# A decoder step on one core: a shared operand slot, two feed-forward tiles kept on chip, one pair of fetches issued later

## The chip, the cores and the metric

The kernel is one program on 1 core of a Trainium2 chip. The metric is the device time of a run in microseconds (us). Its engines are PE (matmuls), ACT and DVE (element-wise work), POOL (some element-wise work, and the DMA queue for transfers that accumulate) and SP (the DMA queue for loads). Every engine carries out its own instructions in order, and waits on semaphores for the others.

## The reference

One layer of a decoder over 512 prompt tokens and 64 sample tokens, `D_MODEL` 1024, everything in float32. The first half (projection, short convolution, windowed attention, mixing) is not touched. The second half, the feed-forward part with `D_FF` 2816, is:

```python
h2 = _rmsnorm(x, norm2_g) * (1.0 + sc2) + sh2
a, val = jnp.split(h2 @ w_up, 2, axis=-1)
ac, new_ffn = _causal_conv(a, ffn_buf, ffn_conv_w)
x = x + g2 * ((jax.nn.gelu(ac, approximate=False) * val) @ w_down)
```

## The kernel before, in words

Channels lie on the 128 partitions and the 576 tokens (`NT`) along the free axis. The 2816 feed-forward channels are 22 tiles of 128. For each tile m the "up" job makes the gate and the value, and their product t, a 128x576 tile of float32 (288 KB). The "down" jobs multiply those tiles by `w_down` and add to the residual.

A float32 product is done in three passes with numbers split into a high and a low part: high x high, high x low, low x high. The high part is an ACT copy into a rounded type, the low part the difference. Up jobs 4 to 21 and most down jobs are "pairs" (`pair_product`): two outputs, two halves of the tokens (a: columns 0 to 287, b: 288 to 575) and two halves of the contraction are done in seven products in place of eight. For this the operands are summed and subtracted first. In PE's queue the seven run one after the other as X, Z, Y, X, Y, Z, Y, after the three PSUM banks that they fill. An up pair has 84 matmuls of 288 columns, a down pair 63.

What stands beside the products is written out by hand: `steps[n]` is a list of small functions that are called after product n - 1 (`steps[0]` before the first), and PE, ACT, DVE and POOL keep this program order. The order of SP's queue, and the placing of tiles in buffers, are found at build time from a simulated timeline. The weights of the next pair are prepared in these steps. Of its four operand parts A, B, C and D, the low half of B and D is made by a POOL DMA that adds the raw weights to the negated high part (in rows: `wlo<-raw` for B and `wl<-s` for D); all else is done by ACT and DVE. In a down pair (k0, 0), the weight work is `sums1` (DVE: `s<-raw,raw`, then `raw<-raw`), `bh` (ACT: `whi<-raw`), `al` (DVE), `bl` and so on.

The order of the jobs: up 4 to 10; the four down pairs (0, 0), (0, 2), (0, 4), (0, 6), which use tiles 0 to 5; up 11 to 16; the down pairs (6, 0) to (6, 6), which use tiles 6 to 11; up 17 to 21; then the rest of down. The operands of a group of down pairs are made in the up jobs before it, two tiles (one k pair) at a time, by `RawOperands`: `sums` (DVE, three operations on the tiles), `first`, `second`, `third` (ACT, high parts) and `first_low` and so on (DVE). `third` of the third k pair runs at the start of (k0, 0). The seventh product's operand, `n4`, is only 288 columns wide. So `third` takes two slots for it, one for high and one for low, and two k pairs share them; the third k pair is alone in a second pair of slots and fills half of each.

"Slots" are one pool of 58 buffers of 128x576 float32 (`A_BUFS`). A tile gets a buffer that another tile had, and its first writer then waits for the last user of that one. The tiles in `KEPT` stay in their slots until a down job uses them. The others are written to DRAM (`away`) by a POOL DMA in the step `high`, and fetched again by an SP DMA (`fetch`): 10 tiles go away and 10 come back. For the last up job before a group of down pairs (`up_last`, tiles 10 and 16) the convolution, GELU and product run in down pairs (k0, 2) and (k0, 4).

The functions that the change touches:

Of the kernel before, what the change touches and what calls it, by code (L numbers as in the profile page):

```python
# [11 lines left out]
F32R = mybir.dt.float32r  # L12
# [15 lines left out]
PAIRED = 6  # L28
PLAIN_AT, LAST_AT = 12, 16
CHUNKS = {0: 10, 6: 16}  # L30
KEPT = (0, 1, 2, 3, 4, 5, 11, 17, 18, 19, 20, 21)
LATE = 2
ROWS_AHEAD = 5
PLAIN = (0, 1, 2, 4, 5, 6)
# [42 lines left out]
def step_kernel(ctx: ExitStack, tc: tile.TileContext, ins: dict, outs: list):  # L77
# [15 lines left out]
    def nm(s):  # L93
        cnt[0] += 1
        return f"{s}{cnt[0]}"

    def slot(s, dt=F32, shape=None):
        return ap_.tile(shape or [P, NT], dt, tag="a", name=nm(s))
# [4 lines left out]
    def aux():  # L103
        return pa.tile([P, 512], F32, tag="aux", name=nm("aux"))
# [3 lines left out]
    class InOrder:  # L108


        def __init__(self, engine):
            self.engine = engine
# [134 lines left out]
    class PairOperands:  # L247
# [21 lines left out]
        def high(self):  # L269
            made, (h0, l0), (h1, l1) = self.made, *self.x  # L270
            self.th, self.tl = slot("th", F32R), slot("tl", F32R)
            act.activation(self.th, self.t, AF.Copy)
            if self.kp % 2 == 0:
                made["n4"] = slot("nh", F32R), slot("nl", F32R)
            a, b = slice(0, HT), slice(HT, NT)
            at = (a, b)[self.kp % 2]
            nh, nl = made["n4"]
            self.nh, self.nl = nh[:, at], nl[:, at]
            act.activation(self.nh, self.r[0][:, a], AF.Copy)
            for name, hi, lo, c in (  # L280
                ("x00", h0, l0, a), ("n3", h0, l0, b), ("x10", h1, l1, a), ("x11", h1, l1, b),
                ("n1", self.th, self.tl, a), ("t2", self.th, self.tl, b), ("n4", nh, nl, at),
            ):
                made.setdefault("op", {}).setdefault(name, []).append((hi[:, c], lo[:, c]))
# [89 lines left out]
    class RawOperands:  # L374

        def __init__(self, r0, r1, made):
            self.r0, self.r1, self.made = r0, r1, made
            made.setdefault("op", {})  # L380

        def put(self, name, hl, c):
# [34 lines left out]
        def third(self):  # L417
            a, b, made = slice(0, HT), slice(HT, NT), self.made
            self.x1 = slot("xh", F32R), slot("xl", F32R)
            act.activation(self.x1[0], self.r1, AF.Copy)  # L420
            self.put("x10", self.x1, a)
            self.put("x11", self.x1, b)
            n = len(made["op"].get("n4", []))
            if n % 2 == 0:
                made["n4"] = slot("nh", F32R), slot("nl", F32R)
            at = (a, b)[n % 2]
            self.n4 = tuple(x[:, at] for x in made["n4"])
            act.activation(self.n4[0], self.r0[:, a], AF.Copy)
            self.put("n4", made["n4"], at)

        def third_low(self):
            self.low(self.x1, self.r1)
# [463 lines left out]
    made = {}  # L896
# [15 lines left out]
    for i in (3, 4):  # L912
        a = aux()
# [24 lines left out]
    def queries(t, ps=None, scale=HD**-0.5):  # L938
# [53 lines left out]
        op=ALU.mult,  # L992
# [488 lines left out]
    for at, m in enumerate(PLAIN):  # L1481
# [25 lines left out]
        if at == 1:  # L1507
            a = aux()
# [329 lines left out]
    class FfnTile:  # L1838
# [43 lines left out]
        def high(self):  # L1882
            if self.m in KEPT:
                kept[self.m] = self.t
# [128 lines left out]
    made2, made_d, kept = {}, {k0: {} for k0 in (*CHUNKS, LAST_AT)}, {}  # L2013
# [75 lines left out]
    ops_d, fs, ops, up_last = {}, {}, {}, {}  # L2089

    def raw_op(k0, kp, *names):
        def f():
            at = k0 + 2 * kp
            if at not in ops_d:
                ops_d[at] = RawOperands(kept.pop(at), kept.pop(at + 1), made_d[k0])
            for name in names:
                getattr(ops_d[at], name)()
        return f

    def fetch(*ms):  # L2100
        def f():
            for m in ms:
                kept[m] = slot("cy")
                nc.sync.dma_start(kept[m], away[m])
        return f
# [36 lines left out]
    order, first_ops = [], {}  # L2142
# [18 lines left out]
                                7: [lambda k0=k0: up_last[k0].high()]},  # L2161
        })
    calls = lambda f, *xs: [lambda x=x: f(x) for x in xs]
    first_ops["down", (0, 6)] = {4: [fetch(6, 7)]}
    first_ops["up", 12][3] = [fetch(8, 9)]
    first_ops["up", 14][3] = [fetch(10)]
    first_ops["up", 17] = {2: [fetch(12, 13)]}
    for at, m in ((18, 12), (19, 14), (20, 16)):
        first_ops["up", at] = {
            2: [fetch(*((14, 15), (16,), ())[at - 18])], 4: calls(down_high, m), 5: calls(down_low, m),  # L2170
            6: calls(down_high, m + 1), 7: calls(down_low, m + 1),
        }
    first_ops["up", 21] = {
# [5 lines left out]
    for n, at in enumerate(order):  # L2179
# [7 lines left out]
        if n + 2 < len(order):  # L2187
            kind, m = order[n + 2]
# [176 lines left out]
```

## Time and profile before

| what | value |
|---|---|
| median of 3 runs | 954.85 us (953.62 to 957.12) |
| the profiled execution, its own time | 955.27 us |
| its span, first to last instruction | 953.5 us |
| mean granted clock of PE | 0.996 |
| PE busy | 936.5 us, 98% of the span |
| DVE, ACT, POOL busy | 739.7, 600.5, 199.8 us |
| DMA | 166.74 MB, of it 50.58 MB on POOL's queue (q0) and 114.41 MB on SP's (q1) |

Times in rows are in us from the first instruction. A row of the timeline gives the start, the duration, engine and line, operation, `out<-in` by the names of the tiles and, in brackets, how long the engine had been idle before it and what ended that. Most operations carry line 116, since one helper records them; so they are told apart by their tiles. In the timeline the up jobs 4 to 10 end at 687.3, the first four down pairs run to 722.9, up 11 to 16 from there to some 790, and the second four down pairs to some 824.

### The profile page before, as it was taken

What the parts mean: (1) busy time and instruction counts of PE and PEld (TensorE: products, weight loads), DVE (VectorE), ACT (ScalarE), POOL (GpSimd) and SP (SyncE); (2) the same over time, 40 slices, a digit from 0 to 9 for tenths busy, and PEclk for the clock granted to TensorE, in tenths of its full rate; (3) what the DMA queues carried; (4) which work ended last, traced back from release to release, by engine and by line L of the source; (5) the groups of instructions that cost most, each with busy time, mean ns of one, the idle gap of its engine ahead of it and who ended that gap; (6) DMA issues with size and microseconds to landing.
All of it is one profiled execution on the core that took longest, in us unless ns stands there. A gap on an engine that the chain in (4) does not pass through costs nothing. (4 is left out here: it accounts for less than half of the span.)

```text
span 953.5 us, 19148 instructions
## 1 busy us (share of the span) xinstructions
PE 936.5 (98%) x7227; PEld 901.4 (95%) x7227; DVE 739.7 (78%) x1395; ACT 600.5 (63%) x1158; POOL 199.8 (21%) x426
## 2 busy tenths in 40 slices
PE   7999999999999999999999999999999999999996
PEld 5799999898999989999889999999999999999996
DVE  4788988875866767876677688888888889877965
ACT  5474768656665446875335567577766776677574
POOL 2222120101111011210001231122243233421131
PEclk9999999999999999999999999999999999999998
DMA  9984233516545768899884832368679877986643
GB/s 281 329 252 109 70 101 98 157 70 151 141 130 171 248 217 214 213 248 291 278 289 122 184 102 67 96 137 198 164 153 233 207 169 167 228 211 151 143 97 105
DMA packets 190032, 166.74 MB, mean 175 GB/s; under 512 B 9177, under 2 KB 162973, under 8 KB 189651
## 3 DMA queue, kind: packets, MB, share of 16 engines
q1 hardware_dynamic: 172210, 114.41, 40.3%
q0 software_dynamic: 17440, 50.58, 24.8%
q8 instruction: 57, 0.93, 0.4%
q10 hardware_dynamic: 288, 0.52, 0.1%
q14 instruction: 37, 0.30, 0.1%
HBM read 116.84 MB, written 15.02 MB: 138 GB/s over the span
## 5 line engine op out<-in xcount | busy, mean ns | idle before, releaser
L116 ACT ACTIVATE whi<-raw 128x1024 fp32r<-128x1024 f32 (+3 forms) x198 | 195.4, 996 | 35.7 <-DVE raw L116 18.0
L116 DVE TENSOR_TENSOR wlo<-raw,whi 128x1024 fp32r<-128x1024 f32 (+3 forms) x153 | 176.1, 1156 | 33.9 <-ACT whi L116 33.4
L116 POOL DMA_DIRECT2D wlo<-raw x45 | 39.0, 866 | 207.2 <-PE mm L116 96.2
L116 DVE TENSOR_TENSOR raw<-raw 128x512 f32<-128x512 f32 (+1 forms) x104 | 69.2, 665 | 3.4
L116 PE MATMUL aux<-2h,whi 128*128 128x288 f32 (+2 forms) x232 | 63.5, 294 | 0.0
L116 PE MATMUL aux<-2l,whi 128*128 128x288 f32 (+2 forms) x232 | 63.5, 295 | 0.0
L116 PE MATMUL mm<-hh,whi 128*128 128x256 f32 (+2 forms) x264 | 60.4, 304 | 0.5 <-ACT hh L116 0.5
L116 PE MATMUL mm<-hl,whi 128*128 128x256 f32 (+2 forms) x264 | 57.3, 297 | 0.0
L116 PE MATMUL mm<-hh,wlo 128*128 128x256 f32 (+2 forms) x264 | 55.4, 295 | 0.0
L116 PE MATMUL aux<-hl,whi 128*128 128x288 f32 (+1 forms) x196 | 53.3, 298 | 0.0
L116 PE MATMUL aux<-hh,whi 128*128 128x288 f32 (+1 forms) x196 | 53.2, 297 | 0.0
L116 POOL DMA_DIRECT2D wl<-s x41 | 35.6, 867 | 71.4 <-ACT wl L116 53.6
L116 ACT ACTIVATE mm<-aux 128x288 f32<-128x288 f32 x49 | 19.5, 397 | 46.7 <-PE aux L116 46.6
L116 ACT ACTIVATE wlo<-whi 128x1024 fp32r<-128x1024 f32 (+1 forms) x45 | 45.4, 1009 | 0.4
L116 PEld LDWEIGHTS mm<-hh,whi 128*128 128x128 f32 x264 | 43.8, 189 | 1.5 <-ACT hh L116 1.0
L116 PEld LDWEIGHTS mm<-hl,whi 128*128 128x128 f32 x264 | 44.1, 188 | 0.9 <-DVE hl L116 0.9
L116 PEld LDWEIGHTS aux<-2l,whi 128*128 128x128 f32 x232 | 43.6, 188 | 0.0
L116 PEld LDWEIGHTS mm<-hh,wlo 128*128 128x128 f32 x264 | 43.6, 188 | 0.0
L116 PEld LDWEIGHTS aux<-2h,whi 128*128 128x128 f32 x232 | 43.5, 188 | 0.0
L116 PE MATMUL aux<-2h,wlo 128*128 128x288 f32 (+2 forms) x232 | 42.1, 295 | 0.0
L1034 ACT ACTIVATE s<-s,nmx 128x256 f32<-128x256 f32 (+1 forms) x72 | 34.0, 477 | 9.6 <-DVE nmx L1028 8.9
L116 ACT ACTIVATE aux<-mm 128x288 f32<-128x288 f32 x52 | 20.6, 396 | 30.6 <-PE mm L116 29.5
(420 smaller groups left out, 3119.2 us busy)
## 6 DMA issues: line engine op xcount, KB each, us to landing
raw<-in_w_in SPq DMA_DIRECT2D x52, 512.0 KB, 4.8
raw<-in_w_up SPq DMA_DIRECT2D x44, 512.0 KB, 4.1
wlo<-raw POOLq DMA_DIRECT2D x34, 512.0 KB, 4.8
ada<-in_w_ada SPq DMA_DIRECT2D x64, 256.0 KB, 5.4
raw<-in_w_down SPq DMA_DIRECT2D x44, 192.0 KB, 3.4
ad<-in_w_ada SPq DMA_DIRECT2D x32, 256.0 KB, 6.2
wl<-s POOLq DMA_DIRECT2D x30, 256.0 KB, 4.3
sg_dram<-sg POOLq DMA_DIRECT2D x16, 288.0 KB, 4.3
```

Of the source, the lines that this page charges most:

```text
L116: done = getattr(self.engine, name)(*args, **kwargs)
L1034: nc.scalar.activation(s[x // 2][:, x % 2, :w], s[x // 2][:, x % 2, :w], AF.Exp, bias=nmx[:, x : x + 1], accum_out=den[:, x : x + 1],)
```

## The change

Three edits. `third` gives the operand `n4` of the third k pair one slot of its own, high part in columns 0 to 287 and low part in 288 to 575 of it, in place of two half-used slots. Tiles 10 and 16 join `KEPT`: their writes to DRAM and their fetches (in up 14 and in up 19) go. The fetch of tiles 6 and 7 moves from step 4 to step 6 of down pair (0, 6), and the `sums` that use them move from step 2 to step 4 of up 11.

```diff
-KEPT = (0, 1, 2, 3, 4, 5, 11, 17, 18, 19, 20, 21)
+KEPT = (0, 1, 2, 3, 4, 5, 10, 11, 16, 17, 18, 19, 20, 21)
...
             n = len(made["op"].get("n4", []))
-            if n % 2 == 0:
-                made["n4"] = slot("nh", F32R), slot("nl", F32R)
-            at = (a, b)[n % 2]
-            self.n4 = tuple(x[:, at] for x in made["n4"])
+            if self.alone:
+                x = slot("nh", F32R)
+                self.n4 = x[:, a], x[:, b]
+            else:
+                if n % 2 == 0:
+                    made["n4"] = slot("nh", F32R), slot("nl", F32R)
+                self.n4 = tuple(x[:, (a, b)[n % 2]] for x in made["n4"])
             act.activation(self.n4[0], self.r0[:, a], AF.Copy)
-            self.put("n4", made["n4"], at)
+            made["op"].setdefault("n4", []).append(self.n4)
...
-                ops_d[at] = RawOperands(kept.pop(at), kept.pop(at + 1), made_d[k0])
+                ops_d[at] = RawOperands(kept.pop(at), kept.pop(at + 1), made_d[k0], kp == PAIRED // 2 - 1)
...
-    first_ops["down", (0, 6)] = {4: [fetch(6, 7)]}
+    first_ops["down", (0, 6)] = {6: [fetch(6, 7)]}
+    first_ops["up", 11][4] = first_ops["up", 11].pop(2)
     first_ops["up", 12][3] = [fetch(8, 9)]
-    first_ops["up", 14][3] = [fetch(10)]
...
-            2: [fetch(*((14, 15), (16,), ())[at - 18])], 4: calls(down_high, m), 5: calls(down_low, m),
+            2: [fetch(*((14, 15), (), ())[at - 18])], 4: calls(down_high, m), 5: calls(down_low, m),
```

How it moves instructions and their waits. In the rows below a name ends in the number of its tile, and brackets hold the semaphores that an instruction waits on: an engine's name, DMASW0 to 7 for POOL's transfers, DMAHW0 to 7 for SP's.

First DVE and ACT at the start of down pair (0, 0). Here `cy1376` is tile 9, whose write to DRAM signals on DMASW1; `nl1388` is the low part of the third k pair's `n4`, `s` and `raw` are the sums of the next pair's weights, and `p5` is the scratch into which ACT copies the second product of (0, 0). DVE before, and DVE after:

```order
L116 TENSOR_TENSOR nl1388_8807<-cy1268_8025,nh1387_8806 128x288 [waits DVE_49,Activation_49]
L116 TENSOR_TENSOR s31391_8824<-raw1357_8642,raw1358_8645 128x384 [waits DMAHW2_49,DMAHW0_49,DMASW1_49]
L116 TENSOR_TENSOR raw1358_8645<-raw1358_8645 128x384 [waits DMAHW3_49,DVE_49]
L116 TENSOR_TENSOR wlo1390_8822<-raw1357_8642,whi1389_8821 128x768 [waits DMAHW1_49,Activation_49]
L116 TENSOR_TENSOR raw1357_8642<-raw1357_8642,raw1358_8645 128x384 [waits DMASW4_49,DVE_49]
```

```order
L116 TENSOR_TENSOR nh1387_8806<-cy1268_8025,nh1387_8806 128x288 [waits DMASW0_49,Activation_49]
L116 TENSOR_TENSOR s31390_8823<-raw1357_8642,raw1358_8645 128x384 [waits DMAHW2_49,DMAHW0_49,DVE_49]
L116 TENSOR_TENSOR raw1358_8645<-raw1358_8645 128x384 [waits DMAHW3_49,DVE_49]
L116 TENSOR_TENSOR wlo1389_8821<-raw1357_8642,whi1388_8820 128x768 [waits DMAHW1_49,Activation_49]
L116 TENSOR_TENSOR raw1357_8642<-raw1357_8642,raw1358_8645 128x384 [waits DMASW4_49,DVE_49]
```

The order is the same; the low part now lies in the slot of the high part, and `s` no longer waits on DMASW1 but only on an earlier DVE instruction. ACT at the same place, before and after:

```order
L116 ACTIVATE mm1382_8800<-aux1381_8799 128x288 [waits PE_49]
L116 ACTIVATE whi1389_8821<-raw1357_8642 128x768 [waits DMAHW1_49,DMAHW0_49]
L116 COPY p51384_8802<-aux1383_8801 128x288 [waits DVE_49,PE_49]
L116 ACTIVATE whi1392_8838<-raw1358_8645 128x768 [waits DMAHW3_49,DVE_49]
L116 ACTIVATE aux1383_8801<-mm1382_8800 128x288 [waits PE_49,Activation_49]
```

```order
L116 ACTIVATE mm1382_8800<-aux1381_8799 128x288 [waits PE_49]
L116 ACTIVATE whi1388_8820<-raw1357_8642 128x768 [waits DMAHW1_49,DMAHW0_49]
L116 COPY p51384_8802<-aux1383_8801 128x288 [waits DMASW1_49,PE_49]
L116 ACTIVATE whi1391_8837<-raw1358_8645 128x768 [waits DMAHW3_49,DVE_49]
L116 ACTIVATE aux1383_8801<-mm1382_8800 128x288 [waits PE_49,Activation_49]
```

The wait on DMASW1 now stands at ACT's copy of the second product, in the buffer that tile 9 had.

Then SP around the fetch of tiles 6 and 7 (`cy<-away`), between the raw weights of up 12 and up 13, before and after:

```order
L155 DMA raw1437_9145<-in_w_up 128x8x128 [waits DMAHW3_49,DMASW6_49,DMAHW6_49,DVE_49,Activation_49]
L155 DMA raw1438_9147<-in_w_up 128x8x128 [waits DVE_49]
L2104 DMA cy1447_9204<-away_7376 128x576 [waits DMASW0_49,DVE_49,DMAHW0_49,PE_49,Pool_49]
L2104 DMA cy1448_9206<-away_7376 128x576 [waits DMAHW1_49,DMASW3_49,PE_49]
L155 DMA raw1455_9255<-in_w_up 128x8x128 [waits DMAHW2_49,DMASW1_49,DMAHW5_49,DVE_49,Activation_49]
```

```order
L155 DMA raw1436_9143<-in_w_up 128x8x128 [waits DMAHW3_49,DMASW6_49,DMAHW6_49,DVE_49,Activation_49]
L155 DMA raw1437_9145<-in_w_up 128x8x128 [waits DVE_49]
L2107 DMA cy1452_9239<-away_7376 128x576 [waits DMAHW0_49,DMASW0_49,PE_49]
L2107 DMA cy1453_9241<-away_7376 128x576 [waits DMASW5_49,DMASW3_49,DMAHW1_49,DVE_49,Pool_49]
L155 DMA raw1454_9253<-in_w_up 128x8x128 [waits DMAHW2_49,DMASW0_49,DMAHW5_49,DVE_49,Activation_49]
```

In SP's own queue the fetches stand where they stood. Their buffers are others, and so their waits: tile 6 waits for a matmul, tile 7 for DVE and POOL operations that read the buffer's former tile. In the built program the PE wait of tile 6 is for the second matmul of the third product of (0, 6), the DVE wait of tile 7 for the second multiply of tile 10 (`cy<-p,y`), and the DMASW waits of both for older transfers.

Last POOL at the same place, before and after; `away<-cy1436` is the write of tile 10, `wlo` the transfer of B for the weights of up 11:

```order
L116 TENSOR_TENSOR rt1435_9127<-p51424_9037,modT_186 128x64 [waits DVE_49]
L116 TENSOR_TENSOR x11070_6533<-x11070_6533,rt1435_9127 128x64 [waits Pool_49]
L116 DMA away_7376<-cy1436_9130 128x576 [waits DMASW0_49,DVE_49]
L116 DMA wlo1446_9168<-raw1420_9032 128x1024 [waits DMASW4_49,DMASW1_49,DMAHW5_49,PE_49,Activation_49]
L1235 MEMSET pad1457_9259 128x2 [waits PE_49]
```

```order
L116 TENSOR_TENSOR rt1434_9126<-p51423_9036,modT_186 128x64 [waits DVE_49]
L116 TENSOR_TENSOR x11070_6533<-x11070_6533,rt1434_9126 128x64 [waits Pool_49]
L116 DMA wlo1445_9166<-raw1419_9031 128x1024 [waits DMASW4_49,DMASW0_49,DMAHW5_49,PE_49,Activation_49]
L1238 MEMSET pad1456_9257 128x2 [waits DVE_49]
L1860 COPY pad1456_9257<-stF_6334 128x8x2
```

The write of tile 10 is gone from in front of B's transfer.

More of the change, by code (lines that the diff above doesn't have):

```diff
@@ L374, in step_kernel, with __init__ @@
     class RawOperands:
-        def __init__(self, r0, r1, made):
-            self.r0, self.r1, self.made = r0, r1, made
+        def __init__(self, r0, r1, made, alone=False):
+            self.r0, self.r1, self.made, self.alone = r0, r1, made, alone
             made.setdefault("op", {})
```

## The prediction

> **What bounds the kernel now.** I read the page first, then what PE waited for, then the stages, then the timeline around each wait.
>
> ```profile
> PE 936.5 (98%) x7227; PEld 901.4 (95%) x7227; DVE 739.7 (78%) x1395; ACT 600.5 (63%) x1158; POOL 199.8 (21%) x426
> ```
>
> PE is busy for 936.5 of 953.5 us, and the change leaves its matmuls as they are. So it can gain only idle time of PE, and only in the feed-forward part. What PE waited for between 545 and 930 us:
>
> ```profile
> PE mm L116 <- ACT aux L116: 1.8, 1, 1.8
> PE aux L116 <- DMA wlo<-raw: 0.6, 1, 0.6
> ```
>
> Two waits, once each, are all. The busy time by stage says where (columns: PE, PEld, DVE, ACT, POOL busy, clock, DMA share, GB/s): the first four down pairs, up 11 to 16, and the second four down pairs.
>
> ```profile
> 687.30:722.90 35.60, 33.76 (x255) 33.52 (x254) 31.41 (x54) 24.98 (x42) 14.11 (x26) 1.00 0.74 183
> 722.90:790.00 67.10, 66.54 (x503) 66.31 (x502) 56.12 (x98) 47.99 (x78) 20.26 (x45) 1.00 0.82 194
> 790.00:826.00 36.00, 36.00 (x273) 36.00 (x272) 33.89 (x58) 25.41 (x43) 14.89 (x28) 1.00 0.79 186
> ```
>
> The first stage lacks 1.84 us, the second 0.56, the third, which does the same work on other tiles, nothing. The clock is full in all three. The most that the change can give is therefore 1.84 + 0.56 = 2.40 us, a quarter of a per cent. I call 0.5% (4.8 us) the least that a measurement of this kernel tells from no change.
>
> **The first wait: one slot fewer in (0, 0).** The chain of waits, then DVE and ACT at this place:
>
> ```profile
> 686.14 5.52 DMA away<-cy
> ...
> 689.19 0.45 DVE L116 TENSOR_TENSOR nl<-cy,nh 128x288 fp32r<-128x288 f32 x1
> 691.68 0.56 DVE L116 TENSOR_TENSOR s<-raw,raw 128x384 f32<-128x384 f32 x1 [2.04 <-DMA away<-cy]
> 692.27 0.56 DVE L116 TENSOR_TENSOR raw<-raw 128x384 f32<-128x384 f32 x1
> ...
> 689.87 0.40 ACT L116 COPY p<-aux 128x288 f32<-128x288 f32 x1
> 692.86 0.84 ACT L116 ACTIVATE whi<-raw 128x768 fp32r<-128x768 f32 x1 [2.60 <-DVE raw L116]
> 693.61 0.39 ACT L116 ACTIVATE aux<-mm 128x288 f32<-128x288 f32 x1
> ...
> 694.06 0.40 PE L116 MATMUL mm<-xh,wh 128*128 128x288 f32 x1 [1.84 <-ACT aux L116]
> ```
>
> Tile 9 is written to DRAM from 686.14 to 691.66. DVE's sum `s` gets its buffer and waits 2.04 us for it; `raw` comes after `s`, ACT's `whi` after `raw`, ACT's `aux` after `whi`, and PE needs `aux`. With the shared slot the order rows show `s` free of that transfer: the buffer that the low half of `n4` had taken goes to `s`. But the wait for tile 9 isn't gone. The next tile that asks for a buffer, `p5`, gets tile 9's, and ACT's copy `p<-aux`, which started at 689.87, now waits for the same landing. Behind it in ACT's queue stand `whi` and `aux`, so PE still waits for them, by a shorter way. Step by step on the old times: `s` follows `nl` at 689.66 and `raw` ends near 690.8, long enough ahead. The copy starts at 691.68, the instant at which DVE got the buffer. What follows such a copy on ACT is read at another place, where nothing is waited for:
>
> ```profile
> 717.08 0.39 ACT L116 COPY p<-aux 128x288 f32<-128x288 f32 x1
> 717.35 1.07 ACT L116 ACTIVATE wlo<-whi 128x1024 fp32r<-128x1024 f32 x1
> ```
>
> Start to start that is 0.27; I take 0.3. So `whi` starts at 691.98 in place of 692.86, `aux` 0.75 later as before (692.86 to 693.61), and PE 0.45 after that (693.61 to 694.06), at 693.18. The gain is 694.06 - 693.18 = 0.88, less an estimated 0.02 for one wait more in ACT's queue: 0.86. Of the 1.84 some 0.98 stays, now under ACT's copy. Nothing ahead of this place changes, so the landing should stand where it stood. Bounds: 0, if ACT resumes much later than DVE did, and 1.84, if tile 9 lands 1.8 us sooner. I take the value between, as the rows of this very place give it.
>
> **The second wait: B of up 11.** PE stops after 8 of the 12 matmuls of the second product, since the low part of B hasn't landed:
>
> ```profile
> 725.32 0.29 PE L116 MATMUL aux<-tl,whi 128*128 128x288 f32 x1
> 726.17 0.53 PE L116 MATMUL aux<-th,wlo 128*128 128x288 f32 x2 [0.56 <-DMA wlo<-raw]
> ...
> 718.73 7.40 DMA wlo<-raw
> ...
> 716.96 0.81 SPq L2104 DMA_DIRECT2D cy<-away  x2
> 717.12 0.38 DVE L116 TENSOR_TENSOR cy<-p,y 128x224 f32<-128x224 f32 x1
> 717.80 0.60 POOL L116 DMA_DIRECT2D away<-cy  x1 [0.79 <-DVE cy L116]
> ```
>
> PE would have gone on at 725.6; B, issued at 718.73, lands at 726.12. Ahead of it stand the two fetches (SP, 716.96) and the write of tile 10 (POOL, 717.80). What the two queues moved from 717.8 to 721.0, then from 721.0 to 726.2 (packets, MB, share of the engines):
>
> ```profile
> q1 hardware_dynamic: 1101, 0.77, 89.1%
> ...
> q0 software_dynamic: 343, 1.05, 88.7%
> q1 hardware_dynamic: 163, 0.31, 15.4%
> ```
>
> Until 721.0 no packet of POOL's queue moves at all; then it moves 1.05 MB in 5.2 us, 0.2 MB a us, first tile 10, then B. Two edits act on this. The write of tile 10 (128x576 float32, 0.295 MB) goes: 0.295 / 0.2 = 1.5 us off B's landing. The fetches are to come behind B, and there the order rows say otherwise. Nothing on SP waits for B: tile 6 now needs a matmul of about 717.1, tile 7 the multiply that ends at 717.50. They issue at some 717.2 and 717.6 in place of 716.96 and 717.4, and still ahead of B. So I give that edit nothing. B then lands at 726.12 - 1.5 = 724.6, a us before PE needs it, and the 0.56 us go. The twin of this place in the second group has the write (tile 16) and no fetch:
>
> ```profile
> 819.14 0.61 POOL L116 DMA_DIRECT2D away<-cy  x1 [1.09 <-DVE x L116]
> 819.75 0.89 POOL L116 DMA_DIRECT2D wlo<-raw  x1
> ...
> wlo<-raw POOLq DMA_DIRECT2D x1, 512.0 KB, 5.3
> ```
>
> B takes 5.3 us there, so without fetches ahead it would be even safer. Bounds: 0 to 0.56; a landing 0.56 us sooner is enough, so I take 0.56.
>
> A rule speaks against this term. The Trainium skill ("SBUF — State Buffer", section "SBUF: two separate sides", its warning on DVE) says that GpSimd can't write the descriptors of its own transfers while DVE runs an operation that takes the port they share, so that such a transfer looks slow without any traffic in its way. By that rule B's 7.4 us would be DVE's doing, tile 10's write would not matter, and the sum below would be 0.86 in place of 1.42. The twin, with the same DVE work beside it and no fetches, took 5.3, which the rule doesn't explain; I keep the traffic.
>
> **What costs nothing.** Two writes and two fetches fewer, 1.2 of 166.74 MB, none of which PE waited for but tile 10's. The `sums` in up 11 change places with DVE's two `raw` sums:
>
> ```profile
> 726.99 0.45 DVE L116 TENSOR_TENSOR tw<-cy 128x288 f32<-128x288 f32 x1
> ...
> 727.90 0.46 DVE L116 TENSOR_TENSOR tw<-cy,tw 128x288 f32<-128x288 f32 x1
> ...
> 728.99 0.69 DVE L116 TENSOR_TENSOR raw<-raw 128x512 f32<-128x512 f32 x1
> 731.86 0.52 DVE L116 TENSOR_TENSOR pad<-mm,p 128x224 f32<-128x224 f32 x2 [2.17 <-ACT xh L116]
> ...
> 733.17 0.29 PE L116 MATMUL mm<-nh,whi 128*128 128x288 f32 x1
> ```
>
> The five operations end at 729.7 either way, and DVE idles 2.17 us behind them. Tiles 10 and 16 hold a slot longer. The place where that is nearest to costing is (6, 0): ACT's copy `p<-aux` there waits, after the change, for tile 15's write, as its twin waits for tile 9's.
>
> ```profile
> 792.93 0.40 ACT L116 COPY p<-aux 128x288 f32<-128x288 f32 x1
> ...
> 789.18 0.58 POOL L116 DMA_DIRECT2D away<-cy  x1 [0.96 <-DVE cy L116]
> ...
> away<-cy POOLq DMA_DIRECT2D x1, 288.0 KB, 3.1
> ```
>
> It lands at 792.3, 0.6 us before the copy. That cover is thin: a write that takes 5.5 us, as tile 9's did, would land at 794.7, and the copy be 1.8 us late, with up to that at PE.
>
> **Sum.** 955.27 - 0.86 - 0.56 = 953.85 us for the profiled execution. That one lies 0.42 above the median of 954.85, so against the median: 953.4 us.
>
> **Rivals.** (1) Both waits go, 2.40 us: 952.4 us. For it: the same kind of write took 3.1 us at 789.18, and tile 9 has to land within 3.7 us of its issue. Against: nothing ahead of it changes. (2) Only the first gain: B is slow for a cause on POOL's or DVE's side, or the fetches alone make it late. Then 0.86, 954.0 us. Against: POOL's queue demonstrably moves tile 10 first. (3) Slower: SP holds the fetches behind B on the chip, as the change's words have it. Then they are issued near 726.1, and a transfer between the slots and `away` lasts up to 7.5 us:
>
> ```profile
> DMA to landing us min/median/max: 3.1/5.2/7.5
> ```
>
> They land at 733.6; the `sums` (1.37 us) and `pad` (0.52) follow, to 735.5, and PE, which starts the next product at 733.17, is 2.4 us late. Net 1.0 us slower: 955.8 us. It decides for slower once tile 7 lands after some 732.6 (731.2, from where PE waits at all, and 1.4 that the rest gains). Against: SP's rows have no wait on B. (4) Only the slot does nothing: ACT resumes as late as DVE did and only B's wait goes, 0.56: 954.3 us. For it: `p5` takes the wait over; against: the copy stands later in the chain than `s`, with two DVE sums cut out.
>
> **How the numbers follow.** Forecast 0.57, (1) 0.12, (2) 0.12, (3) 0.06, (4) 0.09. All five lie within 0.5% of 954.85, and 0.04 are left for what I don't see. The range runs from (1) to (3), 952.4 to 955.8, and 0.4 us beyond either, since a median of runs that spread from 953.62 to 957.12 isn't surer than that: 952.0 to 956.2. More than 0.5% faster would need idle time of PE that isn't there: 0.01. More than 0.5% slower would need a wait of over 6 us that no row hints at: 0.03.
>
> **What would show it.** ACT's `p<-aux` in (0, 0) idle until tile 9's landing, DVE's `s` not; PE's wait there near 1.0 us. B of up 11 in about 6 us with no PE wait; two fetches issued before it all the same; eight writes and eight fetches in all. I am wrong if PE waits at (0, 0) for 1.8 us or for none, if B still holds it, or if a new wait stands in (6, 0).

## The result, and the profile after

The changed kernel takes 952.74 us in the median of 17 runs, the kernel before 954.41 in 17 runs beside it. One of the 17 runs of the changed kernel, 1011.97 us at a granted clock of 0.851, is left out of the ratio. The ratio is 0.9977, with a 95% interval of 0.9969 to 0.9984: 2.2 us, and at least 1.5; the medians differ by 1.7. The forecast was 953.4 us, in a range of 952.0 to 956.2, with no difference of 0.5%, and the result agrees. But the sum behind it had 1.42 us, and the way there was less straight than it said.

The profiled execution spans 951.3 us in place of 953.5. PE's busy time has not moved. Columns as before:

```profile
PE 936.6 (98%) x7227; PEld 901.2 (95%) x7227; DVE 740.1 (78%) x1395; ACT 600.8 (63%) x1158; POOL 201.3 (21%) x424
```

What PE waited for between 545 and 930 us, with the two rows of before (1.8 and 0.6) in mind:

```profile
PE mm L116 <- ACT aux L116: 0.6, 1, 0.6
```

The wait for B is gone, and the one at (0, 0) has shrunk. The stages, over the same stretches as before:

```profile
687.30:722.90 35.60, 35.04 (x265) 34.81 (x264) 32.86 (x57) 25.00 (x42) 14.92 (x26) 1.00 0.78 191
722.90:790.00 67.10, 67.10 (x509) 67.10 (x509) 57.06 (x99) 48.85 (x81) 20.23 (x45) 1.00 0.81 190
790.00:826.00 36.00, 36.00 (x274) 36.00 (x273) 33.84 (x58) 25.00 (x42) 14.80 (x27) 1.00 0.78 178
```

The first lacks 0.56 us in place of 1.84, the second nothing in place of 0.56. Now the timeline at the start of (0, 0):

```profile
686.70 0.58 POOL L116 DMA_DIRECT2D away<-cy  x1 [0.96 <-DVE cy L116]
...
690.12 0.55 DVE L116 TENSOR_TENSOR s<-raw,raw 128x384 f32<-128x384 f32 x1
...
691.83 0.40 ACT L116 COPY p<-aux 128x288 f32<-128x288 f32 x1 [1.41 <-DMA away<-cy]
...
692.13 0.85 ACT L116 ACTIVATE whi<-raw 128x768 fp32r<-128x768 f32 x1
...
692.87 0.41 ACT L116 ACTIVATE aux<-mm 128x288 f32<-128x288 f32 x1
...
693.33 0.40 PE L116 MATMUL mm<-xh,wh 128*128 128x288 f32 x1 [0.56 <-ACT aux L116]
```

DVE's `s` waits for nothing, ACT's copy `p<-aux` waits 1.41 us for tile 9, and the chain behind it is 0.30 + 0.74 + 0.46 = 1.50 us, as forecast. What differs is the copy's start: 691.83 is 5.13 us after the issue of tile 9's write, where DVE got the buffer 5.54 us after it before (686.14 to 691.68). B of up 11, in the timeline:

```profile
716.56 0.86 SPq L2107 DMA_DIRECT2D cy<-away  x2
...
718.01 0.87 POOL L116 DMA_DIRECT2D wlo<-raw  x1 [1.72 <-ACT aux L116]
...
724.72 0.69 PE L116 MATMUL aux<-th,wlo 128*128 128x288 f32 x4
```

The two fetches still go out ahead of B, the first by 1.5 us. B's landing, by its row in the DMA issues, is 6.2 us after its issue, near 724.2; PE takes it at 724.72 without a stop. And (6, 0):

```profile
787.64 0.58 POOL L116 DMA_DIRECT2D away<-cy  x1 [0.96 <-DVE cy L116]
...
791.73 0.40 ACT L116 COPY p<-aux 128x288 f32<-128x288 f32 x1 [0.38 <-DMA away<-cy]
```

There the copy waits 0.38 us for tile 15, and PE does not notice.

One more place differs, at which no edit was aimed: the end of the program. The last output write (`out<-yo`, on ACT's queue), with the packets of instructions behind its issue, before (948.62 to 953.4 us) and after (947.0 to 951.3):

```profile
q14 instruction: 1, 0.01, 0.4%
...
out<-yo ACTq DMA_DIRECT2D x1, 256.0 KB, 3.9
...
out<-yo ACTq DMA_DIRECT2D x1, 256.0 KB, 3.0
```

Before, a packet of instructions starts 2.2 us after the issue, inside the write; after, none starts before it has landed. From that issue to the end of the span it is 4.8 us before and 4.3 after, so 0.5 us of the 2.2 in the span come from here. The later profiles agree: with the program of before, also without its seven warm-up matmuls or with 12 matmuls more, the write takes 3.9 us and the packet lies inside it; in all ten profiles of versions that have at least one of the edits it takes 3.0, and the end is 0.5 to 0.9 us shorter. That the packet is what holds the write, and why the edits move it, was not tested.

### The profile page after: what moved, and what is told of

It reads as the page before. It is cut to its first block, busy times and chain, and to the rows that moved or that the text cites. A ratio compares the mean times of both kernels' runs of the same rounds, so it can differ in the third digit from the quotient of the medians.

```text
span 951.3 us, 19133 instructions
## 1 busy us (share of the span) xinstructions
PE 936.6 (98%) x7227; PEld 901.2 (95%) x7227; DVE 740.1 (78%) x1395; ACT 600.8 (63%) x1158; POOL 201.3 (21%) x424
```

## The experiments

Ratios are against the kernel before, on the same chip, with 95% intervals in brackets. The question was first which edit carries which gain, then why the same instruction waits in one profile and not in the next.

**Each edit by itself.** The shared slot alone:

```
-            self.n4 = tuple(x[:, at] for x in made["n4"])
+            if self.alone:
+                x = slot("nh", F32R)
+                self.n4 = x[:, a], x[:, b]
...
```

> Of the three edits only the shared operand slot is left; tiles 10 and 16 go to DRAM and come back, and the fetch of tiles 6 and 7 stands where it stood. Theory (the two gains are separate, each with its own edit): at (0, 0) DVE's s is free, ACT's copy waits for tile 9's landing instead, and PE waits 0.5 to 1.0 us there in place of 1.84; B of up 11 still holds PE for 0.4 to 0.8 us. Together 0.9 to 1.3 us faster than before, a ratio of 0.9986 to 0.9991. Rival (what counts is the number of transfers, and the slot only hands a wait from DVE to ACT): PE waits 1.8 us at (0, 0) as before, ratio 1.000.

Measured 0.9986, 1.3 us (interval 0.9977 to 0.9995). PE's waits, and ACT's copy:

```profile
PE aux L116 <- DMA wlo<-raw: 1.0, 1, 1.0
PE mm L116 <- ACT aux L116: 0.6, 1, 0.6
```

```profile
693.29 0.40 ACT L116 COPY p<-aux 128x288 f32<-128x288 f32 x1 [1.43 <-DMA away<-cy]
```

The theory holds at (0, 0). Not all of the 1.3 us need be its doing: in this profile the end of the program, behind the issue of the last output write, is 0.9 us shorter than before. At B, PE waits a little longer than the 0.8 us allowed for. Then tiles 10 and 16 alone:

```
-KEPT = (0, 1, 2, 3, 4, 5, 11, 17, 18, 19, 20, 21)
+KEPT = (0, 1, 2, 3, 4, 5, 10, 11, 16, 17, 18, 19, 20, 21)
...
-    first_ops["up", 14][3] = [fetch(10)]
...
-            2: [fetch(*((14, 15), (16,), ())[at - 18])], 4: calls(down_high, m), 5: calls(down_low, m),
+            2: [fetch(*((14, 15), (), ())[at - 18])], 4: calls(down_high, m), 5: calls(down_low, m),
```

> Only tiles 10 and 16 stay on chip; the operand takes two slots and the fetch of tiles 6 and 7 stands where it stood. Theory: DVE's s waits some 2.0 us for tile 9 and PE 1.8 us at (0, 0), as before; B of up 11 lands 6 us or so after its issue and PE does not wait for it: 0.6 to 0.8 us faster than before, ratio 0.9992 to 0.9994. Rival (the fetches ahead of B make it late, not the write): B still takes about 7 us and PE waits 0.3 to 0.6 us for it, ratio 0.9997 to 1.000.

Measured 0.9973 (0.9953 to 0.9994): a wide interval, and a middle at the whole gain. PE has no wait between 545 and 930 us, neither for B, as the theory had it, nor at (0, 0), which it had wrong. In the timeline `s` gets tile 9's buffer at once, 3.4 us after the write's issue, though the program makes it wait for that write as before:

```profile
686.22 0.58 POOL L116 DMA_DIRECT2D away<-cy  x1 [0.95 <-DVE cy L116]
...
689.64 0.55 DVE L116 TENSOR_TENSOR s<-raw,raw 128x384 f32<-128x384 f32 x1
```

So tile 9 landed 2.5 us sooner than in the profile of before (3.0 us after its issue in place of 5.5), and the wait that edit one was to cure was not there. Next the change without its third edit:

```
-    first_ops["down", (0, 6)] = {6: [fetch(6, 7)]}
-    first_ops["up", 11][4] = first_ops["up", 11].pop(2)
+    first_ops["down", (0, 6)] = {4: [fetch(6, 7)]}
```

> The changed kernel with the fetch of tiles 6 and 7 and the sums put back where they were. Theory (that edit does nothing, since the fetches are issued ahead of B either way): as the changed kernel, ratio 0.9977 within 0.0008, one PE wait of about 0.6 us at (0, 0), none at B. Rival (the edit carries the gain at B): PE waits 0.3 to 0.6 us for B again, ratio 0.9981 to 0.9984.

Measured 0.9973 (0.9961 to 0.9984), as the changed kernel: moving the fetch brings nothing that can be measured. No wait at (0, 0) either here, though the program is the changed one up to that place.

**Tile 9 kept too.** The changed kernel, with one tile more on chip:

```
-KEPT = (0, 1, 2, 3, 4, 5, 10, 11, 16, 17, 18, 19, 20, 21)
+KEPT = (0, 1, 2, 3, 4, 5, 9, 10, 11, 16, 17, 18, 19, 20, 21)
...
-    first_ops["up", 12][3] = [fetch(8, 9)]
+    first_ops["up", 12][3] = [fetch(8)]
```

> The changed kernel with tile 9 kept on chip too, so neither written nor fetched. Theory (what is left at (0, 0) is ACT's copy that waits for tile 9's write): that wait and PE's 0.56 us go, PE has no wait between 545 and 930 us, ratio to before about 0.9971. Rival (one slot fewer makes another instruction wait for an older transfer or reader): a new wait of PE of 0.5 us or more in up 11 to 16, ratio 0.9977 or above.

Measured 0.9974 (0.9963 to 0.9984). PE has no listed wait between 545 and 930 us, so nothing took the place of the one removed; the time can't be told from the changed kernel's.

**What makes tile 9 late.** In the profile of before, the DMA queues while tile 9's write is under way show this, from 689.2 to 690.4 us and from 690.4 to 691.3 (packets, MB, share of the 16 engines):

```profile
q1 hardware_dynamic: 469, 0.23, 64.0%
q8 instruction: 1, 0.02, 6.1%
q0 software_dynamic: 4, 0.00, 2.7%
...
q1 hardware_dynamic: 9, 0.00, 1.9%
q0 software_dynamic: 2, 0.00, 1.7%
```

One packet of instructions, 16 KB, fills one of the 16 DMA engines (6.1% is one sixteenth) for the whole first stretch. In the second, with the engines all but empty, two packets of POOL's queue still go out: the last of tile 9. There are 57 such packets in the span, one about every 17 us, and they come at the same PE instructions (within some ten) in every profile; so I took them for loads of PE's program. If such a load holds the write, fewer PE instructions ahead of it will move the load, and the landings with it. Seven warm-up matmuls near 20 us feed nothing; both kernels were run without them:

```
-WARM = 2, 5
+WARM = 0, 0
```

> The kernel before without its seven warm-up matmuls on the identity near 20 us, which feed nothing: PE's program is 28 instructions shorter there, so every 16 KB load of PE instructions comes some 1.9 us later in the work (one comes every 17 us or so). Theory (tile 9's write is held at (0, 0) by such a load, which in the profile of before runs from 3.1 to 4.2 us after the write's issue): the load comes 4.2 to 5 us after the issue, tile 9 lands in 3.0 to 3.6 us, DVE's s and PE do not wait at (0, 0); B of up 11 still holds PE 0.4 to 1.0 us. Some 1.8 us faster than before, ratio 0.998 (0.9972 to 0.9990 if the missing warm-up costs nothing or up to 1 us). Rival (the weight loads beside it, 0.57 MB, make the write slow): it takes 5.0 to 5.5 us, PE waits 1.8 us, ratio 1.000.

> The changed kernel without the same seven warm-up matmuls. Theory (the instruction load holds the write): tile 9 lands in 3.0 to 3.6 us, ACT's copy and PE do not wait at (0, 0), and PE has no wait over 0.5 us between 545 and 930 us; 0.5 to 0.7 us faster than the changed kernel and only 0.5 to 1.0 us faster than the kernel before with the same seven left out, so the slot edit is worth nothing here. Rival (the slot edit shortens the chain whatever the load does): PE waits 0.6 us at (0, 0), and the distance to the kernel before without the seven stays at 2.0 us or more.

The cleanest reading is at tiles 6 and 14, where PE waits for neither. Of the kernel before, the loads and landings at tile 6 (issue 652.78; DMA from 652.7 to 656.5) and tile 14 (issue 778.23; DMA from 777.6 to 778.2, then the write):

```profile
q8 instruction: 1, 0.02, 1.5%
away<-cy POOLq DMA_DIRECT2D x1, 288.0 KB, 6.3
...
q8 instruction: 1, 0.02, 9.3%
...
away<-cy POOLq DMA_DIRECT2D x1, 288.0 KB, 3.2
```

The load falls into tile 6's write, and it starts before tile 14's is issued. Of the kernel before without the seven, the same two writes (issues 654.00 and 778.93; DMA from 653.9 to 654.3, from 659 to 660 and from 778.9 to 780.5):

```profile
away<-cy POOLq DMA_DIRECT2D x1, 288.0 KB, 5.0
...
q8 instruction: 1, 0.02, 6.7%
...
q8 instruction: 1, 0.02, 3.7%
away<-cy POOLq DMA_DIRECT2D x1, 288.0 KB, 4.5
```

The load has moved behind tile 6's landing and into tile 14's write, and tile 6 lands in 5.0 us in place of 6.3, tile 14 in 4.5 in place of 3.2. In the changed kernel the pair goes from 6.6 and 3.2 to 4.9 and 4.9. So at these two tiles the load holds the write that it falls into. All profiles agree at tile 6: 6.3 to 7.1 us in the twelve where the load starts inside the write, 5.0 and 4.9 in the two where it starts behind the landing.

Tile 9 took 3.8 us in both shifted kernels, a little over the forecast 3.0 to 3.6, and PE had no listed wait at (0, 0). But at tile 9 the load isn't the whole account. In nine of the profiles in which PE's program is the same up to there, it starts 2.3 to 3.1 us after the issue, ahead of the landing. In four of them the write took 4.2 to 5.5 us (before, before again, slot only, after), in the other five 3.0 to 3.4. With tiles 10 and 16 only, in the 3.1 us from the issue on:

```profile
q8 instruction: 1, 0.02, 3.1%
...
away<-cy POOLq DMA_DIRECT2D x1, 288.0 KB, 3.0
```

What decides there whether the write is held is not shown; the profile doesn't say which of the 16 engines a packet took.

The times: 0.9984 (0.9973 to 0.9995) and 0.9960 (0.9946 to 0.9975), so the two stay some 2.3 us apart, where the theory said 0.5 to 1.0. The rival had the distance right for a wrong reason. What keeps them apart is B, for which PE waited in the kernel before without the seven

```profile
PE aux L116 <- DMA wlo<-raw: 1.7, 1, 1.7
```

and not at all in the changed one. The wait at (0, 0) was gone and the one at B three times that of the first profile. So each kernel was profiled once more.

> The kernel before, unchanged, profiled once more. Theory (whether the instruction load hits the last packets of tile 9's write differs from execution to execution): the load comes 2.3 to 3.2 us after the write's issue again, and the landing is either 3.0 to 3.5 us with no PE wait at (0, 0) or 5.0 to 5.6 us with 1.4 to 1.9. Rival (the landing belongs to the program): 5.4 to 5.6 us and 1.8 us again.

PE's waits in it, and DVE's `s`:

```profile
PE aux L116 <- DMA wlo<-raw: 1.3, 1, 1.3
PE mm L116 <- ACT aux L116: 0.5, 1, 0.5
```

```profile
690.90 0.56 DVE L116 TENSOR_TENSOR s<-raw,raw 128x384 f32<-128x384 f32 x1 [0.68 <-DMA away<-cy]
```

Tile 9 landed in 4.2 us: between the two cases of the expectation, but not the 5.5 of the program's first profile. The same program waited 1.84 + 0.56 us in one execution and 0.5 + 1.3 in another.

> The changed kernel once more, timed beside the others. Theory (the wait of ACT's copy at (0, 0) depends on whether the instruction load hits tile 9's write): PE waits there for the landing less 4.50 us, that is 0 when tile 9 lands in 3.0 to 4.5 us and 0.5 to 0.6 when it lands in 5.0 to 5.1; no PE wait over 0.2 us at B; ratio 0.9970 to 0.9980. Rival (the wait belongs to the program): 0.5 to 0.6 us again.

Measured 0.9975 (0.9965 to 0.9984). Tile 9 landed in 3.3 us, ACT's copy did not wait, and PE has no listed wait: the theory's first case.

**Does B land when it will, whatever PE does?** Where (0, 0) waited less, B had waited more. Perhaps the transfers set a fixed time for B. Then PE work put between the two would be free in the kernel before:

```
...
+        for _ in range(pad):
+            matmul(X, w["a0"][0](0), x["x00"][0][0], start=True, stop=True, skip_group_check=True)
...
-            pair_product(self.w, made_d[self.k0]["op"], steps, *mix_outs(self.m, 40))
+            pair_product(self.w, made_d[self.k0]["op"], steps, *mix_outs(self.m, 40), pad=12 * ((self.k0, self.m) == (0, 2)))
```

> The kernel before with 12 matmuls more on PE at the start of (0, 2), copies of its first one that feed nothing: 12 x 0.13 = 1.6 us of PE work between (0, 0) and B of up 11. Theory (B lands at a time that the transfers set, some 39.2 to 40 us after the issue of tile 9's write, whatever PE did in between; PE needs it at 37.5): the 1.6 us are taken from PE's wait for B, which falls to 0 to 0.3 us, and the time stays, ratio 0.9995 to 1.0005 (up to 1.001 where PE already lost 1.8 us at (0, 0)). Rival (B follows its issue, and that follows PE): PE waits for B as without them, 0.6 to 1.7 us, and the 1.6 us are all paid, ratio 1.0017.

> The changed kernel with the same 12 matmuls at the start of (0, 2). Both theories: nothing waits there to take them, so all 1.6 us are paid: ratio to before 0.9990 to 0.9996, and no PE wait for B. By the first theory it is 0.3 to 1.0 us faster than the kernel before with the same matmuls, by the rival 2.0 us or more.

Measured 1.0029 (1.0015 to 1.0043) for the kernel before and 0.9993 (0.9984 to 1.0002) for the changed one. The first theory falls: the 1.6 us are paid, and PE still waits 2.0 us for B. That the two waits share a cause isn't shown; five profiles can have paired them by chance. The kernel before lost more than that in its profile, by PE's clock. Set against the same matmuls without the 12, the first one behind the wait for B starts 1.2 us later (727.32 against 726.17), and those from 732 us on 2.7 us later: 1.5 us were lost in between. Busy time by stretch behind the wait for B, which ends at 727.3 (columns as above, the clock third from the end):

```profile
727.00:728.00 1.00, 0.69 (x5) 0.69 (x6) 0.93 (x3) 0.00 (x0) 0.00 (x0) 1.00 0.13 23
728.00:729.00 1.00, 1.00 (x6) 1.00 (x6) 0.97 (x2) 0.85 (x2) 0.00 (x0) 0.50 0.34 70
...
730.00:731.00 1.00, 1.00 (x6) 1.00 (x5) 0.00 (x0) 0.00 (x0) 0.80 (x2) 0.50 1.16 346
731.00:732.00 1.00, 1.00 (x8) 1.00 (x8) 0.00 (x0) 0.92 (x2) 0.00 (x0) 0.80 1.21 292
```

The changed kernel with the 12 matmuls is some 1.7 us slower than without them on the same chip (0.9993 against 0.9975), where both theories said 1.6. Against both, it waited 0.3 us for B; and it waited 0.5 us at a place that the prediction had called thin, (6, 0):

```profile
789.16 0.58 POOL L116 DMA_DIRECT2D away<-cy  x1 [0.95 <-DVE cy L116]
...
794.26 0.40 ACT L116 COPY p<-aux 128x288 f32<-128x288 f32 x1 [1.39 <-DMA away<-cy]
...
795.75 0.40 PE L116 MATMUL mm<-xh,wh 128*128 128x288 f32 x1 [0.54 <-ACT aux L116]
```

The 12 matmuls had moved the load into tile 15's write, which now took 5.0 us, and ACT's copy waited for it as for tile 9's. In the kernel before with the 12 the load starts inside the same write, 3.0 us after its issue, and the write took 3.8; so here too the load alone doesn't settle it.

**What the fetches cost B.** Both fetches behind B, then one of them (with tile 9 kept):

```
-    first_ops["down", (0, 6)] = {6: [fetch(6, 7)]}
...
+    first_ops["up", 11][0] = [fetch(6, 7)] + first_ops["up", 11].get(0, [])
```

> The changed kernel with the fetch of tiles 6 and 7 moved on to step 0 of up 11; on SP's queue it then stands behind two weight loads that wait for B's landing. Theory (the fetches ahead of B cost it 1 to 1.5 us, but PE needs B only 6.7 us after its issue): B lands 4.9 to 5.6 us after its issue in place of 6.2 to 7.0, PE does not wait for B, the fetches issue near 724 to 726 and land by 731; ratio to before 0.9973 to 0.9980. Rival (fetched that late they hold the sums and so the next product): PE waits 0.5 to 2.4 us in the first products of up 12, ratio 0.998 to 1.000.

> The changed kernel with tile 9 kept on chip too, and of the two fetches only tile 6's in (0, 6), tile 7's in step 0 of up 11 (it is issued behind B's landing). Theory (each 0.295 MB ahead of B costs it some 1 us, and tile 7 is needed by 729.9): B lands 5.3 to 6.0 us after its issue, PE has no wait over 0.2 us between 545 and 930 us, ratio to before 0.9970 to 0.9976, not to be told from the changed kernel. Rival (tile 7 lands too late): PE waits 0.3 to 0.8 us in up 12 as with both fetches behind B, ratio 0.9975 to 0.9982.

Measured 0.9972 (0.9959 to 0.9984) and 0.9975 (0.9963 to 0.9987). B's row among the DMA issues of the first, then of the second:

```profile
wlo<-raw POOLq DMA_DIRECT2D x1, 512.0 KB, 4.6
```

```profile
wlo<-raw POOLq DMA_DIRECT2D x1, 512.0 KB, 5.8
```

That is the theory's order, at about 1 us a fetch. But the rival's wait is there too, 0.5 and 0.6 us. In the first one's timeline the fetches are issued at 723.65, and the `sums` hold the next product:

```profile
723.65 2.09 SPq L2107 DMA_DIRECT2D cy<-away  x2
...
729.80 0.46 DVE L116 TENSOR_TENSOR tw<-cy 128x288 f32<-128x288 f32 x1 [2.55 <-DMA cy<-away]
...
731.89 0.40 PE L116 MATMUL mm<-nh,whi 128*128 128x288 f32 x1 [0.52 <-DVE pad L116]
```

**B in all profiles.** From its row of DMA issues and PE's listed waits:

| ahead of B | B lands after, us | PE waits for it, us |
|---|---|---|
| tile 10's write and two fetches (before, before again, slot only, before without the seven, before with 12 matmuls) | 7.4, 8.2, 7.8, 8.6, 8.8 | 0.6, 1.3, 1.0, 1.7, 2.0 |
| two fetches (after, after again, tiles 10 and 16 only, no move, tile 9 kept, after without the seven, after with 12) | 6.2, 6.7, 6.5, 7.0, 7.0, 6.5, 7.1 | 0, 0, 0, 0, 0, 0, 0.3 |
| one fetch | 5.8 | 0 |
| nothing | 4.6 | 0 |

No version beat the changed kernel measurably: the lowest ratio, 0.9960, is that of the changed kernel without its seven warm-up matmuls, and its interval reaches 0.9975.

## Why the prediction was right or wrong

**The bound.** Right: the matmuls didn't move, and the gain, 1.5 to 3.0 us by the interval, came for the most part out of the waits at (0, 0) and B. What the bound left out is the end of the program, behind PE's last matmul, where 0.5 us went. The 0.5% that it took for the least that can be told was too coarse: the interval reaches less than 0.1% to either side.

**The first wait, mechanism.** Right in every step: the wait went from `s` to ACT's copy, and the chain behind the copy is 1.50 us. Tile 9's buffer free after t us costs PE t - 3.7 before (5.54 and 4.17 us gave 1.84 and 0.5) and t - 4.6 with the shared slot (5.13 and 5.16 gave 0.56 and 0.58; tile 15's 5.10 gave 0.54). The difference, 0.9, is the 0.86 forecast; the 0.02 us in it for one more wait in ACT's queue no run shows by itself.

**The first wait, size.** The step that failed is "the landing should stand where it stood". It differs between executions of one program: 5.5 and 4.2 us before, 5.1 and 3.3 after. So PE's 1.84 us were the largest of what such executions show: five profiles with two slots gave 1.84, 0.5 and three times nothing listed, those with the shared slot 0.56, 0.58 and otherwise nothing. What the slot is worth on average is some 0.3 us by these few profiles (means of 0.47 and 0.16 us); 0.86 it is worth only where tile 9 lands 4.6 us or more after its issue. The prediction called itself wrong if PE waited there "for none": the first profile of the changed kernel has 0.56 us, the second none.

**The second wait.** The price of tile 10's write, 1.5 us, was right: the table's first row has a mean of 8.2 us, the second 6.7. The size of the wait, 0.56, was the mis-sized term: it is the smallest of five profiles, whose mean is 1.3 us. "A us before PE needs it" failed as well: PE takes B 6.7 us after its issue, and with both fetches ahead B takes 6.2 to 7.1, so that the cover is all but used up (without the third edit and with tile 9 kept PE starts on B 0.3 us late, too little to be listed).

**The sum.** By these means the two terms are some 0.3 and 1.3 us, together 1.6, in place of 0.86 + 0.56 = 1.42. The first was about 0.6 too large and the second about 0.7 too small, so that the sum came out near is in part luck: both sizes had been taken from one profile. The third part, 0.5 us at the end of the program, the prediction didn't have; with it the profiles come to some 2.1 us, close to the ratio's 2.2.

**The rule weighed against the second term.** The Trainium skill's section on two sides of SBUF ("SBUF — State Buffer", "SBUF: two separate sides") would have left B as late as it was. DVE's work beside B is the same in the table's first two rows, and B still came 1.5 us sooner; the runs speak for the traffic here.

**The fetch.** Right: still issued ahead of B, and without the edit the time is the same. The rows add the price that the prediction didn't need, about 1 us of B for each fetch.

**The rivals.** (1), both waits gone, is what five of the seven profiles in the table's second row show, and one of the two of the changed kernel itself; the 2.2 us of the ratio lie nearer to its 2.40 than to 1.42, but 0.5 of them came from the end of the program. (3) describes rightly what fetches behind B do, with 0.5 us in place of 2.4, but the change doesn't put them there. (2) and (4) were excluded by the profile after.

**The thin cover in (6, 0).** Right: the copy waits for tile 15, 0.38 us and hidden, and 1.39 us and not hidden in the kernel with the 12 matmuls, where that write took 5.0 us.

## What to carry to other kernels

A wait of a microsecond or two in one profile is one draw: look at the same place in a second execution before a term of a sum is taken from it, above all where the wait ends on a transfer. Gains from such places are hard to tell apart: here one edit alone brought 1.3 us, the other 2.6, all three together 2.2, with intervals that overlap, so whether they add is not shown. Taking tile 10's write out from in front of B brought B sooner in every profile; making the chain at (0, 0) shorter helped only where the late landing happened. And compare the whole span, its end included: here 0.5 us came from a place that neither the edits nor the list of waits pointed at.

## What the runs showed of the hardware

- Packets of 16 KB that the profile calls instructions go through the DMA engines that carry the data, one about every 17 us. They come at the same PE instructions in every profile and moved when PE's program was made shorter, so they are taken for loads of it. One filled one engine for the 1.2 us from 689.2 to 690.4. At two tiles the write into which it fell landed 1.3 us later (tile 6: 6.3 against 5.0; tile 14: 4.5 against 3.2); at tile 9 it was late in four of nine profiles. Where a load falls depends on the number of PE instructions ahead: 28 fewer, far earlier in the program, moved one from 3.2 to 5.5 us after tile 6's issue.
- Transfers issued ahead of B made it late: B took 4.6 us with none, 5.8 with one fetch, 6.7 in the mean with two, 8.2 with two and tile 10's write.
- A packet of instructions on another queue (q14) lay inside the last output write in four profiles, and the write took 3.9 us; in the ten in which it came later, 3.0.
- After a wait of 2.0 us PE's granted clock was 0.50 from 728 to 731 us, and 1.5 us were lost on top of the wait. After waits of 1.84 us in the kernel before and 1.7 without the seven it stayed at 1.00. The Trainium skill ("TensorE: Matmul & The Clock Gate", Part 1) gives an idle window of some 3.4 us as what halves the clock; here the clock fell around shorter listed waits. Near the start, too, it was 0.50 for some 3.4 us in six profiles, around waits of 1.3 to 1.8 us (before: 1.47 us, ended at 16.1, the clock 0.50 from 17 to 20), and stayed at 1.00 after waits of 1.73 (before with 12 matmuls) and 1.86 (no move). So the length of the one wait doesn't settle it, and what does is not shown.
